# One root chain for the keys and the first query half, two longer root steps in place of three, a gate product over four heads, and a new issue order, in a two-layer attention trunk

## The chip, the cores and the metric

The kernel runs on one core of one Trainium2 chip. A core has five engines that run at once: TensorE multiplies matrices (PE in the profile, its weight loads PEld), VectorE (DVE), ScalarE (ACT) and GpSimd (POOL) work on tiles in the core's memory, and SyncE (SP) starts most of the transfers (DMA). Every engine takes its instructions from its own queue, in the order in which the program issued them; an instruction whose input is not there yet holds up everything behind it on that engine. The metric is the device time of one execution in microseconds (us). Three runs of the kernel before gave 298.65, 298.95 and 299.74 us; the median is 298.95.

## The reference

Two layers over 256 tokens of width 1024, 16 query heads and 4 key heads of 64 columns. Each layer takes shift, scale and gate from a condition vector, normalises x by its root mean square, makes queries, keys, values and z with one weight matrix, attends, multiplies by silu(z) and goes back through an output matrix:

```python
for i in range(DEPTH):
    shift, scale, gate = jnp.split(cond @ ada_w[i] + ada_b[i], 3, axis=-1)
    h = rms_norm(x, norm_g[i]) * (1 + scale[:, None, :]) + shift[:, None, :]
    y = nsa_mixer(h, ...) if i % 2 == 0 else moba_mixer(h, ...)
    x = x + gate[:, None, :] * y
...
def rms_norm(x, g):
    y = xf * lax.rsqrt(jnp.mean(xf * xf, axis=-1, keepdims=True) + NORM_EPS)
...
q = partial_rope(rms_norm(q.reshape(B, S, N_HEADS, HEAD_DIM), q_g), cos, sin)
k = partial_rope(rms_norm(k.reshape(B, S, N_KV, HEAD_DIM), k_g), cos, sin)
...
return (o * jax.nn.silu(z)) @ w_out
```

Layer 0 (nsa) has three kinds of keys: compressed blocks (a small network over 32-token windows), selected blocks and a window. With 256 tokens all four blocks are selected, so the last two are causal attention with different keys. Layer 1 (moba) is plain causal attention with one kind of key. Queries and keys are normalised per head of 64 columns, so every token needs one inverse square root for each head.

## The kernel before

The program does not call the engines directly. Every call to `T` (TensorE), `A` (ScalarE), `V` (VectorE), `G` (GpSimd) and `S`/`Q` (SyncE) is written down by `Plan.record` as an operation with a number, 2403 in all. `Plan.issue` then sends them out in the order of the list `ORDER`, which is written out by hand in the file; so a queue's order is the order of that engine's numbers in the list, and all instructions carry the line of the one call in `issue` (L303). Tiles have a tag (`buf`, `part`, `rs`, `g` and so on), and a tag has a fixed number of buffers which are handed out in that same order: a tile whose tag has no free buffer could not be issued there.

All large products are made in pairs of a rounded part and the rest of it (`part`, `HT`, `qg`, `KTA`): ScalarE copies the rounded part, VectorE subtracts to get the rest, and TensorE multiplies three of the four combinations. This subtraction is the largest use of VectorE.

The course of layer 0: the condition's products and the normalised x (0 to 15 us); keys and values of all three kinds with their weights arriving (15 to 80 us, `products_of`); then `make_k` for the selected and window keys, the tiles `FLAT` for the compressed keys (tile `p`, written by VectorE from transposed `KC`), and the products of FLAT with `nsa_cmp_w1` (`cmp_steps`), while `chunk` with `q_and_gates` makes the first eight query heads and the branch gates, and `make_q` turns the heads into `QT`; then the second query half, z, the attention of two pairs of key heads (`pair_a`), `gated` for each pair, and `out_products` with `w_out`. `next_h` (called per half of the tokens) makes h of layer 1. Layer 1 does the same with `make_k` for one kind of key, two `make_q`, z, `pair_b`, `gated` and the last `out_products`.

What the change touches:

`rstd_of(ss, n, inv)` makes an inverse square root out of small VectorE instructions on n columns: two that set up a first guess by bits, then three Newton steps, of three instructions each where n is over 1 and of two where n is 1. So a call has 11 or 8 instructions, and each needs the result of the one ahead of it.

`norm_rope` squares on ScalarE, sums each head on VectorE, calls `rstd_of`, scales and rotates. It is called by `make_k` in layer 0 (16 columns: 2 kinds, 2 token halves, 4 heads), by the first and second `make_q` (16 columns each), once for the compressed keys (1 column), and in layer 1 by `make_k` (8 columns) and two `make_q` (16 each). `rstd_of` with one column also runs twice at the start and twice in `next_h`.

`gated(pair, o, zT)` multiplies the attention output by z. `o` are four tiles in TensorE's output memory, one for each 32-token residue, holding four heads. It takes two heads at a time: four VectorE products into a tile `g` (128x128 each), one ScalarE copy and one VectorE subtraction into `qg`; then the same for the other two heads. `z_blocks` makes z as one `zT` tile for each two heads. The tag `g` has two buffers of 512 columns, `zT` four of 512, `rs` four of 64, `ss` four of 16.

Of the kernel before, what the change touches and what calls it, by code (L numbers as in the profile page):

```python
# [18 lines left out]
P = 128  # L19
# [318 lines left out]
def kernel(  # L338
# [46 lines left out]
    plan.tag("early", early["pool"], 1024, 12)  # L385
    plan.tag("buf", work, 1024, 10)
    plan.tag("part", work, 1024, 10, F32R)
    plan.tag("ss", work, 16, 4)
    plan.tag("rs", work, 64, 4)
    plan.tag("rot", work, 256, 1)  # L390
    plan.tag("rs2", early["pool"], 256, 1)
# [1105 lines left out]
```

## Time and profile before

| | |
|---|---|
| median of three runs | 298.95 us (298.65 to 299.74) |
| the profiled execution | 298.08 us, its span 296.3 us |
| granted TensorE clock | 1.000 |
| ACT busy | 194.6 us (66%) |
| POOL busy | 43.8 us (15%) |
| moved by DMA | 70.83 MB, mean 239 GB/s |

The span goes from the first to the last instruction; 1.78 us of the execution lie outside. An engine's busy time is the time in which at least one of its instructions was running. For TensorE the ends of matmuls are modelled and consecutive matmuls overlap, so it counts as busy a little past the moment at which it could have taken the next one. The profile's groups are named by tile: `rs` holds the root chains, `ss` the sums of squares, `p` is both FLAT and the attention's probabilities, `part` the split weights.

### The profile page before, as it was taken

What the parts mean: (1) busy time and instruction counts of PE and PEld (TensorE: products, weight loads), DVE (VectorE), ACT (ScalarE), POOL (GpSimd) and SP (SyncE); (2) the same over time, 40 slices, a digit from 0 to 9 for tenths busy, and PEclk for the clock granted to TensorE, in tenths of its full rate; (3) what the DMA queues carried; (4) which work ended last, traced back from release to release, by engine and by line L of the source; (5) the groups of instructions that cost most, each with busy time, mean ns of one, the idle gap of its engine ahead of it and who ended that gap; (6) DMA issues with size and microseconds to landing.
All of it is one profiled execution on the core that took longest, in us unless ns stands there. A gap on an engine that the chain in (4) does not pass through costs nothing. (4 is left out here: it accounts for less than half of the span.)

```text
span 296.3 us, 6988 instructions
## 1 busy us (share of the span) xinstructions
PE 286.2 (97%) x2612; PEld 240.8 (81%) x2612; DVE 255.2 (86%) x541; ACT 194.6 (66%) x464; POOL 43.8 (15%) x111
## 2 busy tenths in 40 slices
PE   6999999999989999999999999899999999999994
PEld 6877788799957878879997788678888999897874
DVE  0486899937899999999999999976889999999985
ACT  4283353649514669996899944877584899799410
POOL 8600889960000000000001000000000000000000
PEclk9999999999999999999999999999999999999999
DMA  7999999998939989797967989254878766295003
GB/s 236 318 334 349 352 364 340 357 295 269 318 117 368 385 280 364 231 291 160 270 194 214 227 210 347 89 177 145 283 283 215 204 171 195 74 237 154 2 0 142
DMA packets 48698, 70.83 MB, mean 239 GB/s; under 512 B 4919, under 2 KB 24985, under 8 KB 48666
## 3 DMA queue, kind: packets, MB, share of 16 engines
q1 hardware_dynamic: 48298, 70.34, 77.7%
q8 instruction: 20, 0.33, 0.5%
q14 instruction: 12, 0.10, 0.1%
q0 software_dynamic: 256, 0.02, 0.1%
q10 hardware_dynamic: 112, 0.04, 0.0%
HBM read 67.76 MB, written 2.62 MB: 238 GB/s over the span
## 5 line engine op out<-in xcount | busy, mean ns | idle before, releaser
L303 PE MATMUL ps<-part,HT 128*128 128x512 f32 (+2 forms) x408 | 96.2, 375 | 0.3
L303 PEld LDWEIGHTS ps<-part,HT 128*128 128x128 f32 x408 | 69.1, 188 | 13.0 <-issue 0.8
L303 DVE TENSOR_TENSOR part<-buf,part 128x1024 fp32r<-128x1024 f32 (+2 forms) x58 | 64.0, 1113 | 12.0 <-ACT part L303 10.1
L303 ACT CAST part<-buf 128x1024 fp32r<-128x1024 f32 (+2 forms) x58 | 55.4, 979 | 18.8 <-PE ps L303 11.5
L303 PE MATMUL ps<-HT,part 128*128 128x256 f32 x384 | 62.8, 289 | 0.0
L303 PEld LDWEIGHTS ps<-HT,part 128*128 128x128 f32 x384 | 52.8, 189 | 2.9 <-issue 0.9
L303 PE MATMUL ps<-part,qg 128*128 128x512 f32 (+1 forms) x240 | 49.1, 356 | 0.0
L303 PEld LDWEIGHTS ps<-part,qg 128*128 128x128 f32 x240 | 38.6, 188 | 8.4 <-issue 1.3
L303 ACT ACTIVATE p<-ps,tiny 128x256 f32<-128x256 f32 (+1 forms) x96 | 39.6, 459 | 7.4 <-DVE tiny L303 7.2
L303 PE MATMUL ps<-KTA,qg 128*128 128x256 f32 (+1 forms) x192 | 29.7, 288 | 0.5 <-ACT part L303 0.3
L303 ACT CAST part<-early 128x1024 fp32r<-128x1024 f32 (+1 forms) x16 | 15.0, 938 | 21.5 <-DMA early<-in_nsa_w_in_dram 21.4
L303 PEld LDWEIGHTS ps<-KTA,qg 128*128 128x128 f32 x192 | 25.8, 190 | 1.6 <-ACT part L303 0.4
L303 DVE TENSOR_REDUCE tiny<-ps 128x2 f32<-128x512 f32 (+2 forms) x40 | 24.8, 628 | 1.2 <-PE ps L303 1.0
L303 ACT ACTIVATION_READ_ACCUMULATOR p<-ps,tiny 128x1 f32 x96 | 23.4, 244 | 0.0
L303 DVE STREAM_TRANSPOSE p<-p 128x1536 f32<-128x1536 f32 x12 | 21.0, 1766 | 1.1 <-ACT p L303 0.9
L303 ACT ACTIVATE p<-p,tiny 128x256 f32<-128x256 f32 x48 | 21.8, 585 | 0.1
L303 ACT COPY buf<-ps 128x512 f32<-128x512 f32 (+1 forms) x25 | 11.7, 488 | 12.8 <-PE ps L303 10.1
L303 DVE TENSOR_TENSOR part<-early,part 128x1024 fp32r<-128x1024 f32 (+1 forms) x16 | 17.5, 1100 | 1.9 <-ACT part L303 1.9
L303 PE MATMUL ps<-buf,condz 128*32 128x256 f32 x192 | 11.8, 382 | 0.0
L303 DVE SCALAR_TENSOR_TENSOR sum<-early,condz,sum 128x512 f32<-128x512 f32 x14 | 10.6, 756 | 0.2
L303 POOL MEMSET buf<- 128x1024 f32 x1 | 1.0, 953 | 64.4 <-PE ps L303 64.4
L303 POOL TENSOR_SCALAR rot<-rot 128x16 f32<-128x16 f32 x19 | 10.1, 532 | 1.6
(191 smaller groups left out, 401.7 us busy)
## 6 DMA issues: line engine op xcount, KB each, us to landing
buf<-in_ada_w_dram SPq DMA_DIRECT2D x32, 512.0 KB, 5.7
buf<-in_moba_w_in_dram SPq DMA_DIRECT2D x20, 512.0 KB, 5.4
early<-in_ada_w_dram SPq DMA_DIRECT2D x32, 256.0 KB, 6.1
buf<-in_nsa_w_in_dram SPq DMA_DIRECT2D x12, 512.0 KB, 7.4
early<-in_nsa_w_in_dram SPq DMA_DIRECT2D x8, 512.0 KB, 5.8
buf<-in_nsa_cmp_w_dram SPq DMA_DIRECT2D x8, 512.0 KB, 5.7
buf<-in_nsa_w_out_dram SPq DMA_DIRECT2D x16, 256.0 KB, 8.7
buf<-in_moba_w_out_dram SPq DMA_DIRECT2D x16, 256.0 KB, 5.6
```

The lines of the kernel that those rows point to most:

```text
L303: getattr(self.engines[op["engine"]], method)(*[self._real(a) for a in args], **{k: self._real(a) for k, a in kw.items()})
```

## The change

Five things are edited, and since operations fall away, every number in `ORDER` after them is new; the list now has 2352 entries. The new list is not the old one renumbered: engine by engine it holds the same operations, less those removed, with many of them moved some places forward or back.

First, in `rstd_of` the three Newton steps become one Newton step and one third-order step: 9 instructions where n is over 1 and 7 where it is 1. The rows of the tile grow from 16 to 32 columns. Second, squaring and summing leave `norm_rope` (`square_sums`, `heads_of`), so that in layer 0 the sums of the keys (16 columns) and of the first query half (16) lie side by side in one `tiny` tile and one `rstd_of` call makes the roots of both; the keys are scaled only after that. In layer 1 the same is done with 8 and 16 columns. The second query halves keep a chain of their own. Third, `gated` makes its four products over all four heads (128x256 each) into one `g` tile, and `z_blocks` writes one `zT` tile for four heads. Fourth, the buffers follow: `ss` 2 of 16, `rs` 3 of 96, `zT` 2 of 1024, `g` 1 of 1024. Fifth, the order.

```diff
 ORDER = [
-    2, 1, 3, 0, 4, 49, 42, 43, 44, 51, 41, 48, 50, 45, 18, 19, 20, 21, 22, 16, 23, 24, 25, 26, 27, 28, 29, 30, 53,
...
+    1, 2, 18, 0, 3, 4, 42, 48, 44, 50, 43, 41, 49, 51, 19, 20, 21, 22, 23, 16, 24, 52, 54, 55, 53, 61, 62, 56, 63,
...
-    plan.tag("ss", work, 16, 4)
-    plan.tag("rs", work, 64, 4)
+    plan.tag("ss", work, 16, 2)
+    plan.tag("rs", work, 96, 3)
...
-    ATTN = {"qg": (1024, 4, F32R), "zT": (512, 4, F32), "p": (1536, 4, F32), "vr": (2048, 1, F32),
-            "u": (256, 1, F32), "pc": (256, 2, F32), "g": (512, 2, F32)}
+    ATTN = {"qg": (1024, 4, F32R), "zT": (1024, 2, F32), "p": (1536, 4, F32), "vr": (2048, 1, F32),
+            "u": (256, 1, F32), "pc": (256, 2, F32), "g": (1024, 1, F32)}
...
-        s = tile_of("rs", 3, 16)
-        half, y, a = (s[:q, i, :n] for i in range(3))
-        V.tensor_scalar(half, ss, 0.5 * inv, 0.5 * EPS, op0=OP.mult, op1=OP.add)
-        V.tensor_scalar(y.bitcast(I32), half.bitcast(I32), -0.5, float(1597463007 - 0x400000 - 2 ** 31), op0=OP.mult, op1=OP.add)
-        for _ in range(3):
+        s = tile_of("rs", 3, 32)
+        v, y, a = (s[:q, i, :n] for i in range(3))
+        V.tensor_scalar(v, ss, 64 / 9 * inv, 64 / 9 * EPS, op0=OP.mult, op1=OP.add)
+        V.tensor_scalar(y.bitcast(I32), v.bitcast(I32), -0.5, float(0x5f0b3000 - 2 ** 31), op0=OP.mult, op1=OP.add)
+        for step in range(2):
             if n == 1:
-                V.scalar_tensor_tensor(a, y, half, y, op0=OP.mult, op1=OP.mult)
+                V.scalar_tensor_tensor(a, y, v, y, op0=OP.mult, op1=OP.mult)
             else:
                 V.tensor_mul(a, y, y)
-                V.tensor_mul(a, a, half)
-            V.scalar_tensor_tensor(y, a, -1.5, y, op0=OP.add, op1=OP.mult)
+                V.tensor_mul(a, a, v)
+            if step:
+                V.scalar_tensor_tensor(a, a, -10 / 3, a, op0=OP.add, op1=OP.mult)
+            V.scalar_tensor_tensor(y, a, (-1.8898815748423101, 5.0)[step], y, op0=OP.add, op1=OP.mult)
         return y
...
+    def square_sums(src, dst, ss):
+        A.activation(dst, src, AF.Square)
+        V.tensor_reduce(ss, dst, axis=AX.X, op=OP.add)
+
-    def norm_rope(src, nm, nh, tabC, tabS, dst):
+    def norm_rope(src, nm, nh, tabC, tabS, dst, r):
...
-        A.activation(dst, src, AF.Square)
-        ss = tile_of("ss", 16)[:q, :n]
-        V.tensor_reduce(ss, dst, axis=AX.X, op=OP.add)
-        r = rstd_of(ss, n, 1.0 / HD)
...
-        for acc in accs:
-            t, zT = tile_of("y", 2, S), tile_of("zT", 2, S)
+        zT = tile_of("zT", 4, S)
+        for q, acc in enumerate(accs):
+            t = tile_of("y", 2, S)
             A.activation(t, acc, AF.Tanh, scale=0.5)
-            V.scalar_tensor_tensor(zT, t, 1.0, acc, op0=OP.add, op1=OP.mult)
-            out.append(zT)
+            V.scalar_tensor_tensor(zT[:, 2 * q:2 * q + 2], t, 1.0, acc, op0=OP.add, op1=OP.mult)
+        out.append(zT)
...
+    def heads_of(raw, ss):
+        y = tile_of("buf", ss.shape[1], HD)
+        square_sums(raw, y, ss)
+        return raw, y
...
     def gated(pair, o, zT):
+        t = tile_of("g", 4, S)
+        for a in range(4):
+            sl = [z.rearrange("p j (b i) -> p j b i", b=8)[:, :, a:8 - a:7 - 2 * a] for z in (t, zT[pair])]
+            V.tensor_mul(sl[0], sl[1], o[a].rearrange("p (m h i) -> p h m i", m=2, h=4))
         for q in range(2):
-            t = tile_of("g", 2, S)
-            for a in range(4):
-                sl = [z.rearrange("p j (b i) -> p j b i", b=8)[:, :, a:8 - a:7 - 2 * a] for z in (t, zT[2 * pair + q])]
-                V.tensor_mul(sl[0], sl[1], o[a].rearrange("p (m h i) -> p h m i", m=2, h=4)[:, 2 * q:2 * q + 2])
+            some = t[:, 2 * q:2 * q + 2]
             both = tile_of("qg", 2, 2, S)
...
-            A.copy(both[:, :, 0, :], t)
-            V.tensor_sub(both[:, :, 1, :], t, both[:, :, 0, :].bitcast(F32))
+            A.copy(both[:, :, 0, :], some)
+            V.tensor_sub(both[:, :, 1, :], some, both[:, :, 0, :].bitcast(F32))
...
-    make_k(raw_k, (2, 3), KTA, (256, 384, 128, 0))
+    sums = tile_of("tiny", 32)
+    k_own = k_heads(raw_k, sums[:, 0:16])
...
-    make_q(raw_q, 0, QT, 0)
+    q_own = q_heads(raw_q, sums[:, 16:32])
+    roots = rstd_of(sums, 32, 1.0 / HD)
+    make_k(k_own, roots[:, 0:16], (2, 3), KTA, (256, 384, 128, 0))
+    make_q(q_own, roots[:, 16:32], 0, QT, 0)
...
-    make_k(raw_k, (5,), KTB, (0, P))
+    sums = tile_of("tiny", 32)
+    k_own = k_heads(raw_k, sums[:, 0:8])
...
-    make_q(raw_q, 4, QT, 0)
+    q_own = q_heads(raw_q, sums[:, 8:24])
+    roots = rstd_of(sums[:, 0:24], 24, 1.0 / HD)
+    make_k(k_own, roots[:, 0:8], (5,), KTB, (0, P))
+    make_q(q_own, roots[:, 8:24], 4, QT, 0)
```

More of the change, by code (lines that the diff above doesn't have):

```diff
@@ L803, in raw_part, with k_heads, q_heads, make_k @@
         return done
-    def make_k(raw_k, kinds, kt_view, offs):
+    def heads_of(raw, ss):
+        y = tile_of("buf", ss.shape[1], HD)
+        square_sums(raw, y, ss)
+        return raw, y
+    def k_heads(raw_k, ss):
+        return heads_of(raw_k.rearrange("p c m (g d) -> p (c m g) d", d=HD), ss)
+    def q_heads(raw_q, ss):
+        return heads_of(raw_q.rearrange("p m (h d) -> p (m h) d", d=HD), ss)
+    def make_k(heads, r, kinds, kt_view, offs):
         n = len(kinds)
-        src = raw_k.rearrange("p c m (g d) -> p (c m g) d", d=HD)
-        y = tile_of("buf", 8 * n, HD)
+        src, y = heads
         k0, j0 = kinds[0], (2, 3, 5).index(kinds[0])
         norm_rope(src, 2 * n, KVH, TC[:, j0:j0 + n].rearrange("p c m d -> p (c m) d"),
-                  TS[:, k0:k0 + n].rearrange("p c m d -> p (c m) d"), y)
+                  TS[:, k0:k0 + n].rearrange("p c m d -> p (c m) d"), y, r)
         for j, off in enumerate(offs):
@@ L825, in make_k, with make_q @@
             V.tensor_sub(lo, tv, hi.bitcast(F32))
-    def make_q(raw_q, kind, qt, g0):
-        y = tile_of("buf", 16, HD)
-        norm_rope(raw_q.rearrange("p m (h d) -> p (m h) d", d=HD), 2, 8, TR[:, kind], TS[:, kind], y)
+    def make_q(heads, r, kind, qt, g0):
+        src, y = heads
+        norm_rope(src, 2, 8, TR[:, kind], TS[:, kind], y, r)
         for m in range(2):
@@ L1103 @@
     A.copy(raw_q[:, :, 0:256], q_acc)
-    KC = [[tile_of("zT", KVH, 2 * HD) for m in range(2)] for kv in range(2)]
+    KC = [[both[:, m] for m in range(2)] for both in (tile_of("zT", 2, KVH, 2 * HD) for kv in range(2))]
     for ci in (1, 2, 0):
@@ L1210 @@
     kcy = const.tile([64, 1, HD], F32, name="kcy")
-    norm_rope(kcm[:, None, 0:64], 1, 1, TCc[:, None, :], TSc[:, None, :], kcy)
+    sums = tile_of("tiny", 32)[0:64, 0:1]
+    square_sums(kcm[:, None, 0:64], kcy, sums)
+    norm_rope(kcm[:, None, 0:64], 1, 1, TCc[:, None, :], TSc[:, None, :], kcy, rstd_of(sums, 1, 1.0 / HD))
     kcz = tile_of("part", 1, 2, 2, HD)
@@ L1238, in second_q @@
         chunk(w_in, ((512, 512),), raw_part(raw_q, 512))
-        make_q(raw_q, 0, QT, 2)
+        sums = tile_of("tiny", 32)[:, 0:16]
+        own = q_heads(raw_q, sums)
+        make_q(own, rstd_of(sums, 16, 1.0 / HD), 0, QT, 2)
     SECOND = -1
@@ L1419 @@
     chunk(m_in, ((0, 512),), raw_part(raw_q, 512))
-    make_q(raw_q, 4, QT, 0)
+    q_own = q_heads(raw_q, sums[:, 8:24])
+    roots = rstd_of(sums[:, 0:24], 24, 1.0 / HD)
+    make_k(k_own, roots[:, 0:8], (5,), KTB, (0, P))
+    make_q(q_own, roots[:, 8:24], 4, QT, 0)
     raw_q = tile_of("buf", 2, 512)
     chunk(m_in, ((512, 512),), raw_part(raw_q, 512))
-    make_q(raw_q, 4, QT, 2)
+    sums = tile_of("tiny", 32)[:, 0:16]
+    own = q_heads(raw_q, sums)
+    make_q(own, rstd_of(sums, 16, 1.0 / HD), 4, QT, 2)
     zT = []
```

241 rows, old and new, of the table ORDER are left out of this document.

## The prediction, made before the changed kernel ran

> **What bounds the kernel now.** I read the page's busy times first, then the stages, then what TensorE waits for.
>
> ```profile
> span 296.3 us, 6988 instructions
> ...
> PE 286.2 (97%) x2612; PEld 240.8 (81%) x2612; DVE 255.2 (86%) x541; ACT 194.6 (66%) x464; POOL 43.8 (15%) x111
> ```
>
> TensorE is busy for all but 10.1 us, VectorE for all but 41. The change takes no work from TensorE, so it can only shorten TensorE's waits. Where they lie, a cut of the span into stages says (stage and length; then busy us and instructions of PE, PEld, DVE, ACT, POOL; granted clock; DMA share; GB/s):
>
> ```profile
> 0.00:10.00 10.00, 7.70 (x35) 7.38 (x36) 3.01 (x19) 4.40 (x7) 8.62 (x40) 1.00 0.86 250
> 10.00:70.00 60.00, 59.17 (x425) 48.52 (x424) 43.93 (x86) 30.30 (x46) 33.80 (x70) 1.00 1.07 343
> 70.00:100.00 30.00, 28.47 (x196) 22.60 (x195) 27.79 (x70) 15.04 (x25) 0.40 (x1) 1.00 0.81 270
> 100.00:185.00 85.00, 84.85 (x1141) 71.72 (x1140) 81.51 (x173) 69.14 (x211) 0.95 (x1) 1.00 0.88 259
> 185.00:200.00 15.00, 14.11 (x66) 10.49 (x65) 12.60 (x43) 11.94 (x30) 0.00 (x0) 1.00 0.41 137
> ...
> 215.00:260.00 45.00, 44.48 (x409) 40.49 (x409) 43.01 (x97) 35.55 (x85) 0.00 (x0) 1.00 0.67 191
> 260.00:290.00 30.00, 29.97 (x259) 24.82 (x259) 28.84 (x43) 18.01 (x46) 0.00 (x0) 1.00 0.35 91
> 290.00:296.30 6.30, 2.41 (x17) 2.05 (x15) 3.14 (x7) 0.00 (x0) 0.00 (x0) 1.00 0.46 166
> ```
>
> Of the 10.1 us, 2.30 lie in the first 10 us and 3.89 at the end, where the result is written out. The middle has 3.95: 0.83 while the first weights arrive, 1.53 between 70 and 100, 0.15 in layer 0's attention, 0.89 between the layers, 0.52 between 215 and 260, next to nothing after. In the third and the sixth stage VectorE is 93% and 96% busy: there the two are nearly even.
>
> The busy figure hides part of the waits, because a matmul counts as busy past the start of the next one:
>
> ```profile
> 83.22 0.40 PE L303 MATMUL ps<-part,HT 128*128 128x512 f32 x1
> ...
> 84.94 4.19 PE L303 MATMUL ps<-buf,p 128*64 128x256 f32 x32 [1.32 <-DVE p L303]
> ...
> 89.99 2.00 PE L303 MATMUL ps<-part,HT 128*128 128x512 f32 x8
> ...
> 93.48 0.48 PE L303 MATMUL ps<-part,HT 128*128 128x512 f32 x1
> ...
> 94.17 0.63 PE L303 MATMUL ps<-identF,y 128*128 128x128 f32 x4 [0.21 <-DVE p L303]
> ```
>
> The eight at 89.99, each 0.40 long, start (2.00 - 0.40) / 7 = 0.23 us apart. After the one at 83.22 the next starts 1.72 us later, so 1.49 us are lost, and 1.32 show. After the one at 93.48 it is 0.69, so 0.46 are lost and 0.21 show. Both wait for VectorE's additions into FLAT (tile `p`). I therefore take the lost time in the middle to be up to twice what shows, 7.9 us.
>
> The Trainium skill (Perfetto Trace Analysis, section Identifying the Most-Contended Engine) goes further: matmul busy time is a poor measure of distance from the limit, weight-load busy time a better one. By that rule (81% against VectorE's 86%) VectorE would be the limit and every microsecond taken from it would count; that is the first rival. The two places above speak for the rule, the 10 to 70 row (PE 59.17 of 60, DVE 43.93) against it.
>
> **The change part by part.** VectorE's groups (count, busy us, mean ns of one):
>
> ```profile
> L303 DVE TENSOR_TENSOR g<-zT,ps 128x128 f32<-128x128 f32 x32 | 7.0, 278 | 1.0 <-PE ps L303 1.0
> ...
> L303 DVE TENSOR_TENSOR rs<-rs 128x16 f32<-128x16 f32 x30 | 4.9, 169 | 0.5
> L303 DVE SCALAR_TENSOR_TENSOR rs<-rs 128x1 f32<-128x1 f32 x24 | 4.2, 186 | 0.5
> ...
> L303 DVE TENSOR_TENSOR y<-ps,buf 128x256 f32<-128x256 f32 x4 | 1.7, 420 | 0.2
> ...
> L303 DVE TENSOR_TENSOR rs<-rs 128x8 f32<-128x8 f32 x6 | 1.0, 165 | 0.1
> ...
> L303 DVE TENSOR_TENSOR tiny<-ps,GBIAS 128x48 f32<-128x48 f32 x2 | 0.4, 204 | 0.0
> ```
>
> *Merged chains.* A chain on 16 columns is 11 instructions of about 0.169 us, 1.86 us. In layer 0 two of them (3.72) become one of 9 on 32 columns. That width is not in the trace: it lies between 0.169 (16 columns) and 0.204 (48 columns, read from TensorE's memory). I take 0.18, nearer to the first, as going from 8 to 16 columns costs only 0.004: 1.62, so 2.1 us less (bounds 1.88 and 2.20). In layer 1, 11 x 0.165 and 11 x 0.169 are 3.67; 9 at 0.175 are 1.58, also 2.1 less (1.83 to 2.15).
>
> *Shorter chains.* The two second query halves lose 2 x 0.169 each, 0.68 together. Five one-column chains (two at the start, two in `next_h`, one for the compressed keys) lose one instruction of 0.186 each, 0.93.
>
> *Gate.* Per pair of key heads:
>
> ```profile
> 174.12 9.53 PE L303 MATMUL ps<-part,qg 128*128 128x512 f32 x47
> 174.19 1.67 DVE L303 TENSOR_TENSOR g<-zT,ps 128x128 f32<-128x128 f32 x8 [0.38 <-PE ps L303]
> ...
> 175.30 0.62 ACT L303 CAST qg<-g 128x512 fp32r<-128x512 f32 x1 [3.98 <-DVE g L303]
> 175.96 0.69 DVE L303 TENSOR_TENSOR qg<-g,qg 128x512 fp32r<-128x512 f32 x1
> ```
>
> Eight products take 1.67 us: 0.28 each, 0.08 of it overlapping the next. Four of twice the size at 0.42 take 1.44 with that overlap and 1.68 without: 0.2 us less per pair, 0.8 over four pairs (bounds 0 and 0.9). The first copy into `qg` now waits for all four products: it started 1.11 us after the first product and will start about 1.5 after. TensorE covers the 0.4: it runs 9.53 us without a break from before the products to long after the copy. Behind the waiting copy on ScalarE stand casts of weights for the same output products, under the same cover; without it, it costs 0.4 a pair. The single `g` buffer makes the next pair's products wait for this pair's last subtraction (0.69 each), but the pairs lie far apart, so I cost it at nothing.
>
> *VectorE in all*: 2.1 + 2.1 + 0.68 + 0.93 + 0.8 = 6.6 us: 0.37 at the start, 3.0 between 70 and 185, 0.37 between the layers, 2.84 after 215.
>
> *What reaches TensorE.* Between 71 and 85 us six instructions of the keys' chain stand in VectorE's queue ahead of the additions for which TensorE waits at 84.94 (the keys' sums are ready from 71 on, row below). All go to the merged chain: 6 x 0.169 = 1.0 us of the 1.49; next late is the query half's sum, which stays. Of the 0.46 at 93.48 I take 0.3. From 100 to 185 0.15 us shows idle and VectorE saves 0.9; I take 0.3. Between the layers the chain of `next_h` stands alone on the path:
>
> ```profile
> 188.01 1.05 DVE L303 SCALAR_TENSOR_TENSOR rs<-rs 128x1 f32<-128x1 f32 x5
> ...
> 191.37 0.50 PE L303 MATMUL ps<-KTA,HT 128*128 128x512 f32 x1 [0.88 <-ACT HT L303]
> ```
>
> Five dependent steps take 1.05, so one fewer gives 0.2. From 220 to 240 the chain that ended last runs through VectorE piece by piece (start, length, what; its first root step, one of the middle, and the first score maximum after them):
>
> ```profile
> 220.18 0.16 DVE rs L303
> ...
> 236.35 0.19 DVE rs L303
> ...
> 238.51 0.69 DVE tiny L303
> ```
>
> There VectorE saves 2.4, but TensorE shows only 0.52 idle, at most 1.0 by the doubling: I take 0.8. At the start I take 0.1, because the next stage moves 343 GB/s at a DMA share of 1.07 and its products follow the weights. At the end nothing changes. Sum: 1.0 + 0.3 + 0.3 + 0.2 + 0.8 + 0.1 = 2.7 us.
>
> *The new order* is the unknown. Renumbering the diff's list shows the same 1225 TensorE entries, on average 7 places from where they were and at most 66, so it reshuffles within stages. No row shows its waits. On the good side it is bounded by the 7.9 us lost in the middle; on the bad side by new waits of the size of the largest now, 1.49: three of them would be 4.5. I take zero, since most stretches of either list are the same products in another sequence.
>
> The execution profiled took 298.08 us, so 295.4 after; it lay 0.87 below the median of the runs, 298.95, so **296.2** for the median.
>
> **Rivals.** *VectorE is the bound* and its savings land whole: 6.6 less the 0.37 at the start, 298.95 - 6.2 = 292.7. For it speak the waits on `p` and the chain from 220 to 240; against it 84.85 of 85 us in layer 0's attention.
>
> *TensorE was full*: freed VectorE time turns into idle VectorE time, and a wait that goes comes back behind the next instruction (ScalarE's casts, the weights). Only `next_h` and a little else is gained, 0.5: 298.5, no change by measurement. For it speaks the 97%; against it the 1.49 us, which have a plain cause. A change that did not do what it says would look the same; VectorE's count (541, to be 51 fewer) tells them apart.
>
> *Keys wait for queries*, the slower one. The keys' roots now need the sums of the first query half. In layer 0 sums and scalings stood so, keys first, then queries:
>
> ```profile
> 71.40 1.22 DVE L303 TENSOR_REDUCE ss<-buf 128x16 f32<-128x1024 f32 x1 [0.24 <-ACT buf L303]
> ...
> 82.59 1.20 DVE L303 TENSOR_REDUCE ss<-buf 128x16 f32<-128x1024 f32 x1
> ...
> 87.42 1.21 DVE L303 TENSOR_TENSOR buf<-buf,rs 128x1024 f32<-128x1024 f32 x1
> ...
> 94.36 1.23 DVE L303 TENSOR_TENSOR buf<-buf,rs 128x1024 f32<-128x1024 f32 x1
> ```
>
> Queued behind the merged chain are the keys' rotation, their transposes and the splits into `KTA`, and the scores wait for those. If the keys slip to the queries' place, all this is 6.9 us late. If TensorE covers a third, 4.6 are lost against 1.4 gained elsewhere (0.3 + 0.2 + 0.8 + 0.1): 302.2. It decides once the uncovered delay is over 1.4 us. Against it: the query sums are ready at 83.79, nine steps of 0.2 end near 86, before the keys' scaling at 87.42 now.
>
> **How the numbers follow.** Two such kernels can be told apart from about 0.5%, 1.5 us: faster means under 297.45, slower over 300.45. Chances: forecast 0.45 (a gain of 1.5 to 5), VectorE bound 0.14, TensorE full 0.27, keys late or another wait of the new order 0.14. So faster 0.59, same 0.27, slower 0.14. The range leaves out most of the slower rival and a little below the first: 292.4 to 300.5.
>
> **What would show it.** VectorE with 490 instructions and about 249 us busy; `rs` rows of 32 and 24 columns below 0.2 us; 16 `g` rows of 128x256; TensorE's wait on `p` ahead of the first product with FLAT under 0.6 us; the wait on `HT` between the layers 0.2 shorter. I am wrong if TensorE's idle time in the middle stays near 3.95 us, if new waits on `KTA` or `qg` appear, or if the weights' stage ends at another time than 70 us.

## The result and the profile after

The changed kernel took 302.01 us (median of seven runs, 300.39 to 304.22) and the kernel before 298.45 (297.64 to 299.74): the ratio is 1.0128, 95% interval 1.0089 to 1.0166. It is slower, by 2.7 to 5.0 us, where 2.7 us less were forecast. In some runs of every kernel TensorE stands at half its clock for a window of 3.41 us, which costs about 1.7 us (an estimate, half of the window); five of the seven runs here had one, and the two without took 300.39 and 301.69, so this explains at most a part. The profiled execution took 301.69 us, its span 300.0.

The page of the changed kernel, its busy times:

```profile
span 300.0 us, 6944 instructions
...
PE 287.7 (96%) x2612; PEld 241.9 (81%) x2612; DVE 249.9 (83%) x490; ACT 194.6 (65%) x464; POOL 43.6 (15%) x111
```

VectorE has lost its 51 instructions and 5.3 us of busy time. TensorE does the same 2612 products and is idle longer. The same cut into stages as before (stage and length; busy us and instructions of PE, PEld, DVE, ACT, POOL; granted clock; DMA share; GB/s):

```profile
10.00:70.00 60.00, 59.75 (x431) 48.99 (x431) 43.19 (x80) 31.92 (x49) 33.63 (x70) 1.00 1.03 333
70.00:100.00 30.00, 28.46 (x196) 23.17 (x196) 26.88 (x57) 12.87 (x23) 0.40 (x1) 1.00 0.88 302
100.00:185.00 85.00, 82.15 (x1112) 68.52 (x1111) 76.22 (x155) 68.47 (x209) 0.95 (x1) 1.00 0.84 249
185.00:200.00 15.00, 13.82 (x71) 10.55 (x70) 13.48 (x43) 10.09 (x26) 0.00 (x0) 1.00 0.33 117
...
215.00:260.00 45.00, 44.50 (x394) 39.99 (x393) 43.24 (x76) 36.37 (x83) 0.00 (x0) 1.00 0.71 182
```

The third row is the one to see. Layer 0's attention showed 0.15 us of idle TensorE before and shows 2.85 now, while VectorE's load there fell from 81.51 to 76.22. In the other rows TensorE's idle time differs by 0.6 us at most. VectorE's groups of the change (count, busy us, mean ns of one) came out as priced:

```profile
L300 DVE TENSOR_TENSOR g<-zT,ps 128x256 f32<-128x256 f32 x16 | 5.9, 415 | 2.0 <-PE ps L300 1.8
...
L300 DVE TENSOR_TENSOR rs<-rs 128x32 f32<-128x32 f32 x4 | 0.7, 185 | 0.1
L300 DVE TENSOR_TENSOR rs<-rs 128x24 f32<-128x24 f32 x4 | 0.7, 181 | 0.1
```

Where did TensorE stop? Its timeline, the rows behind a wait (start, length, what, and in brackets the idle time and what ended it; "issue" is a wait for nothing that the profile shows):

```profile
84.96 3.74 PE L300 MATMUL ps<-buf,p 128*64 128x256 f32 x32 [1.54 <-DVE p L300]
...
139.99 0.50 PE L300 MATMUL ps<-HT,part 128*128 128x256 f32 x2 [0.88 <-ACT part L300]
...
161.22 1.93 PE L300 MATMUL ps<-buf,condz 128*32 128x256 f32 x32 [0.33 <-issue]
...
172.53 0.45 PE L300 MATMUL ps<-p,vr 32*64 32x128 f32 x8 [1.22 <-issue]
...
194.78 0.50 PE L300 MATMUL ps<-part,HT 128*128 128x512 f32 x1 [0.79 <-ACT HT L300]
...
196.31 0.51 PE L300 MATMUL ps<-KTA,HT 128*128 128x512 f32 x1 [0.34 <-DVE HT L300]
```

Taken from start to start, as in the prediction, these lose 1.71, 1.23, 0.58, 1.46, 0.94 and 0.50 us. The first was 1.49 before, the last two were one of 1.03, the other three are new: 1.23 + 0.58 + 1.46 + 0.22 + 0.41 = 3.90, against a span that is 3.7 longer. (The sum does not close exactly: the products with the second half of FLAT start 0.73 us earlier than before, at 94.23, and some smaller waits are longer.)

The wait at 139.99 is for a cast on ScalarE, and that cast has a row of its own:

```profile
138.90 2.00 ACT L300 CAST part<-buf 128x1024 fp32r<-128x1024 f32 x2 [2.37 <-DMA buf<-in_nsa_w_in_dram]
```

It waited 2.37 us for z weights. SyncE's queue, which starts the loads (start, time in the queue's engine, what, count):

```profile
120.31 0.39 SPq L300 DMA_DIRECT2D buf<-in_ada_w_dram  x1
120.79 0.42 SPq L300 DMA_DIRECT2D buf<-in_nsa_w_in_dram  x1
121.30 0.42 SPq L300 DMA_DIRECT2D buf<-in_ada_w_dram  x1
...
128.36 0.46 SPq L300 DMA_DIRECT2D buf<-in_nsa_w_in_dram  x1
141.23 1.92 SPq L300 DMA_DIRECT2D buf<-in_nsa_w_out_dram  x3
```

By their numbers in the list, the load at 128.36 is the one that is needed first, at 139; the condition weights at 120.31 and 121.30 are used only at 162 and 161. The next load was issued at 141.23, just after VectorE's subtraction had read the first of the late weights (141.20), so none starts for 13 us. Before, the same z weights were asked for at 122.73 and used at 135.7:

```profile
122.73 0.37 SPq L303 DMA_DIRECT2D buf<-in_nsa_w_in_dram  x1
```

### The profile page after: what moved, and what is told of

It reads as the page before. It is cut to its first block, busy times and chain, and to the rows that moved or that the text cites. A ratio compares the mean times of both kernels' runs of the same rounds, so it can differ in the third digit from the quotient of the medians.

```text
span 300.0 us, 6944 instructions
## 1 busy us (share of the span) xinstructions
PE 287.7 (96%) x2612; PEld 241.9 (81%) x2612; DVE 249.9 (83%) x490; ACT 194.6 (65%) x464; POOL 43.6 (15%) x111
## 5 line engine op out<-in xcount | busy, mean ns | idle before, releaser
L300 PE MATMUL ps<-part,HT 128*128 128x512 f32 (+2 forms) x408 | 97.3, 375 | 0.8 <-ACT HT L300 0.8
L300 PEld LDWEIGHTS ps<-part,HT 128*128 128x128 f32 x408 | 68.3, 188 | 12.9 <-ACT HT L300 1.7
L300 PE MATMUL ps<-HT,part 128*128 128x256 f32 x384 | 65.4, 291 | 0.9 <-ACT part L300 0.9
L300 PEld LDWEIGHTS ps<-HT,part 128*128 128x128 f32 x384 | 53.7, 190 | 4.4 <-ACT part L300 1.2
L300 ACT ACTIVATION_READ_ACCUMULATOR p<-ps,tiny 128x1 f32 x96 | 24.7, 258 | 0.0
L300 ACT ACTIVATE p<-p,tiny 128x256 f32<-128x256 f32 x48 | 22.6, 603 | 0.1
L300 ACT COPY buf<-ps 128x512 f32<-128x512 f32 (+1 forms) x25 | 12.3, 517 | 12.4 <-PE ps L300 12.4
L300 PE MATMUL ps<-p,vr 32*64 32x128 f32 (+1 forms) x368 | 10.1, 298 | 1.4 <-issue 1.4
```

Of the source, the lines that this page charges most:

```text
L300: getattr(self.engines[op["engine"]], method)(*[self._real(a) for a in args], **{k: self._real(a) for k, a in kw.items()})
```

## The experiments

Two questions: is it the edits or the order, and what in the order? The kernels were timed in five sets, each on a chip of its own with the kernel before beside them (298.17 to 298.47 us); the ratios are to that one. A median is known to about 1 us.

**The edits alone**, with the old order. The old list is renumbered, the removed numbers left out, and the merged chains stand where the queries' chain stood.

```diff
 ORDER = [
-    1, 2, 18, 0, 3, 4, 42, 48, 44, 50, 43, 41, 49, 51, 19, 20, 21, 22, 23, 16, 24, 52, 54, 55, 53, 61, 62, 56, 63,
+    2, 1, 3, 0, 4, 49, 42, 43, 44, 51, 41, 48, 50, 45, 18, 19, 20, 21, 22, 16, 23, 24, 25, 26, 27, 28, 29, 30, 53,
...
```

> The changed kernel's four edits of the code with the instruction order of the kernel before: its list renumbered, the removed entries left out, the merged root chains where the queries' chain stood; 50 of the 2352 entries stand elsewhere only because their inputs would not be ready. If the new order is what costs (theory O), the slow-down of 3.6 us goes and what the edits alone gain is seen: 295.8 to 298.5 us, at or a little below the kernel before (298.45), with the new waits at 139 and 171 us gone. If the edits cost (theory E: the keys wait for the queries' sums, the single g buffer), the time stays near the changed kernel's 302 us whatever the order.

298.68 us, ratio 1.0006 (0.9976 to 1.0035), just above the range of theory O and far from theory E. Page and TensorE's timeline of this kernel:

```profile
PE 285.8 (96%) x2612; PEld 240.1 (81%) x2612; DVE 251.1 (85%) x490; ACT 194.7 (66%) x464; POOL 44.1 (15%) x111
```

```profile
84.64 4.13 PE L294 MATMUL ps<-buf,p 128*64 128x256 f32 x32 [0.77 <-DVE p L294]
...
93.63 0.66 PE L294 MATMUL ps<-identF,y 128*128 128x128 f32 x4 [0.72 <-ACT y L294]
```

The slow-down is gone, so it was the order. But nothing is gained either: the wait at FLAT fell from 1.49 to 0.94 us lost, and the next one, at the products that turn the keys (`identF,y`), rose from 0.46 to 0.89. It moved as well: before it was the second group of them (94.17), put down to an addition into FLAT (`p`), now it is the first, which follows ScalarE's copy of the rotated keys (`y`).

**The new order with the old code.** The removed operations are put in beside those that they belong to (the keys' chain directly ahead of the queries'). In the file of the kernel before:

```diff
 ORDER = [
-    2, 1, 3, 0, 4, 49, 42, 43, 44, 51, 41, 48, 50, 45, 18, 19, 20, 21, 22, 16, 23, 24, 25, 26, 27, 28, 29, 30, 53,
+    1, 2, 18, 0, 3, 4, 42, 48, 44, 50, 43, 41, 49, 51, 19, 20, 21, 22, 23, 16, 24, 52, 54, 55, 53, 62, 63, 56, 64, 65,
...
```

> The code of the kernel before (two chains of three Newton steps, gate by two heads) with the changed kernel's order, the operations that the change removed put in beside the ones they belong to. Theory O: 302 to 304 us, as slow as the changed kernel or a little slower, with the waits at 139 and 171 us still there. Theory E: back near 298.5 us.

307.39 us, ratio 1.0303 (1.0254 to 1.0351): slower than foreseen. What TensorE waited for in this kernel (us in total, times, longest):

```profile
PE ps L297 <- DVE part L297: 2.6, 2, 2.0
PE ps L297 <- issue: 2.0, 2, 1.8
PE ps L297 <- ACT part L297: 1.8, 1, 1.8
```

The waits for `part` on ScalarE and for "issue" are the two of the changed kernel, and longer; the first row is new. So in this order old code and edits are 307.39 - 302.01 = 5.4 us apart, and in the old one not measurably. The 5.4 are not the worth of the edits alone, since a part hangs on where the removed operations were put: the longest new wait, 2.05 us at 83.77, ends with a remainder that VectorE began at 82.50, behind the keys' chain as it was put in (from 80.26 on); in the changed kernel that remainder began at 80.27.

**The late load.** Two entries of SyncE's queue are exchanged.

```diff
-    1325, 1076, 1117, 1073,
+    1325, 1028, 1117, 1073,
...
-    1075, 1028,
+    1075, 1076,
```

> The changed kernel with two entries of the order exchanged: the load of the z weights that are needed at 139 us takes the place of a load of condition weights that are needed only at 162 us, and the reverse, so it is issued about 8 us earlier. Theory O, its first part (late z weights): the wait of ScalarE for that load (2.37 us) and TensorE's wait of 1.23 us behind it go, the hole in the DMA traffic from 135 to 141 us closes, and the time falls by 1.2 to 2.0 us to 300.0 to 300.8. Rival: TensorE only meets the next late thing, the time stays within 0.5 us of 302.

301.45 us, ratio 1.0103 (1.0066 to 1.0140). TensorE's timeline:

```profile
138.24 0.58 PE L295 MATMUL ps<-HT,part 128*128 128x256 f32 x2
...
160.23 1.93 PE L295 MATMUL ps<-buf,condz 128*32 128x256 f32 x32 [1.05 <-issue]
```

The wait of 1.23 us is gone as foreseen, but the products with the condition weights now lose 1.29 us where they lost 0.58. TensorE came 1.7 us sooner, and they started only 1.0 us sooner: 0.7 us were given back 20 us later. The time lies between the two expectations, and its interval overlaps that of the changed kernel (1.0089 to 1.0166); the hole in the loads did not close either, with none issued from 128.4 to 139.7. What the trace shows is the wait that went and the one that grew.

**The row of small products.** Nine output products are moved between the two value groups. (In the trace the row of small products counts 136, from 168.59 to 172.71 us, and 68 stand on either side of the nine; the 34 of the recorded texts are the products of one entry of the list.)

```diff
+    1366, 1388, 1367, 1389, 1368, 1369, 1370, 1390, 1391,
     1299,
...
-    1366, 1388, 1367, 1389, 1368, 1369, 1370, 1390, 1391,
```

> The changed kernel with nine 512-wide output products moved, in TensorE's order, from behind to between two groups of 34 small value products at 168 to 173 us, as the kernel before had seven there. Theory F (a long row of small matmuls runs ahead of the fetch of TensorE's instructions): the 1.22 us in which TensorE waited at 171 us for nothing that the profile shows go, and the time falls by 0.8 to 1.3 us to 300.7 to 301.2. Rival: the stall sits at that place for another reason (a semaphore that the profile does not name), it moves with the group, and the time stays within 0.5 us of 302.

300.97 us, ratio 1.0069 (1.0032 to 1.0106). The wait at 171 us is gone, and 1.0 us of the median with it, as theory F has it (the interval still overlaps that of the changed kernel). The counter-test does the reverse to the kernel before (old numbers):

```diff
-    1393, 1415, 1416, 1394, 1395, 1396, 1417,
     1321,
+    1393, 1415, 1416, 1394, 1395, 1396, 1417,
```

> The kernel before with its seven output products between the two groups of 34 small value products (168.9 to 170.7 us) moved behind the second group, so that the groups follow each other as in the changed kernel; nothing else. Theory F (TensorE runs out of instructions, since the block it needs is fetched behind the data transfers): a wait of about 1.4 us in the second group, put down to no releaser, appears, ended some 1.4 us after the block of instructions has landed, and the time is 1.0 to 1.5 us above before, 299.2 to 299.7. Rival: the stall belongs to something else in the changed kernel, and the time stays within 0.4 us of 298.2.

300.01 us, ratio 1.0060 (1.0029 to 1.0091), 0.3 us more than theory F had, and TensorE's timeline has the wait:

```profile
171.45 0.50 PE L297 MATMUL ps<-p,vr 32*64 32x128 f32 x12
173.29 0.45 PE L297 MATMUL ps<-p,vr 32*64 32x128 f32 x9 [1.34 <-issue]
```

It stands in the middle of a row of like products of which twelve had run, so a missing input is unlikely. Counting TensorE's instructions in the trace from the start, beginning with 0, it stands ahead of number 3265 here, and ahead of the same number in the changed kernel, in the one with the early load and in the old code with the new order. The trace also has the packets that bring instructions (queue 8; packets, MB, share), for the changed kernel as a whole and from 170.0 to 171.2 us:

```profile
q8 instruction: 20, 0.33, 0.5%
```

```profile
q1 hardware_dynamic: 233, 0.44, 99.6%
q8 instruction: 1, 0.02, 5.5%
```

Twenty blocks of 16 KB for 5289 instructions of TensorE are 264 for each. In the four kernels that wait, a block landed at 171.16, 170.37, 174.65 and 171.64 us, and TensorE went on at 172.53, 171.76, 176.19 and 173.29: 1.37 to 1.65 us later each time. In the kernel before, the block landed at 169.96 and TensorE came to number 3265 at 171.63, 1.67 us later, without a wait: the seven products between the groups had given the time. The other blocks say the same: counting on from number 3265 in steps of 256, both ways, the first instruction of a block started 1.29 us or more after its block had landed, in each of the 19 blocks that this reaches, in all fourteen traces; in steps of 255 or 257 the shortest time is 1.02 or 0.68. So TensorE runs out of instructions there. A smaller shortage stands in both kernels, at number 2241: in the changed one 0.48 us at 137.27, 1.35 after a landing, and in the kernel before 0.53 at 135.73, 1.41 after a landing. That the block comes late because the data transfers fill the DMA engines (99.6% in the row above) is argued, not shown; its packet took 1.05 us there, and 0.98 us at 278.95, where the DMA share is 0.06, so if they delay it, they delay its start and not the packet itself.

**Three places mended.** The two changes above, and the condition products (1074, 1077) put behind seven and three more output products:

```diff
-    1164, 1074, 1077,
+    1164,
...
+    1379, 1074,
...
+    1351, 1077,
```

> The changed kernel with three places of its order mended together: the exchange of the two loads (z weights early), the nine output products between the two value groups, and the two groups of condition products that waited at 159 to 161 us put behind seven and three output products more. Theory O, in these places: 302.0 less 1.2 (139 us) less 1.2 (171 us) less 0.6 (160 us), that is 298.7 to 299.3. Rival: with these three gone the same time is lost in other places, the time stays over 300.5.

299.29 us, ratio 1.0035 (1.0007 to 1.0063), as theory O has it. Of the 3.33 us between the changed kernel and the edits in the old order, 2.72 are these three places.

**Why do the edits bring nothing in the old order?** The remaining waits were filled with ready products, with the old code and with the edits. In both (new numbers):

```diff
+    766, 774, 775, 767, 768, 769, 770,
     548,
...
+    1888, 1889, 1890, 1891, 1884, 1898,
     2055,
...
+    1988, 1998, 1992,
     2123,
```

> The kernel before, its code unchanged, with the same three moves of TensorE's products (not the move in VectorE's queue). If the moves do all and the edits nothing: 296.7 to 297.5, at most 0.7 us above the edits with the same moves. If VectorE's saving of 4 to 5 us is worth something once the order lets it: 1.0 us or more above that kernel. If TensorE is full: 298.2, no change.

298.48 us, ratio 0.9999 (0.9971 to 1.0027). TensorE's timeline:

```profile
85.19 3.97 PE L297 MATMUL ps<-buf,p 128*64 128x256 f32 x32
...
92.98 0.66 PE L297 MATMUL ps<-identF,y 128*128 128x128 f32 x4 [1.29 <-DVE rs L297]
```

The 1.49 us at FLAT are gone, and 1.46 are lost six microseconds later, for the keys; their second group goes on losing 0.5 as before. With the edits, the same moves and VectorE's chain ahead of the additions for the second half:

> The edits with the order of the kernel before (298.68) and moves at three places: seven output products ahead of the first product with FLAT, where TensorE waits 0.94 us at 83.5; VectorE's merged chain and the keys' rotation ahead of the additions for the second half of FLAT, for TensorE's wait of 0.89 us for the keys at 92.5; six and three products of ready weights ahead of scores that wait 0.61 us at 236.2 and 0.49 us at 252.9. If such waits are real losses that order can fill: 296.0 to 297.0. If TensorE is full and each wait that goes comes back behind the next instruction: within 0.5 us of 298.7.

299.82 us, ratio 1.0028 (0.9994 to 1.0062), in neither range; the profiled execution, at full clock throughout, took 298.58. TensorE's timeline:

```profile
85.21 3.67 PE L294 MATMUL ps<-buf,p 128*64 128x256 f32 x32
...
98.30 0.44 PE L294 MATMUL ps<-identF,g 128*128 128x128 f32 x2 [0.47 <-ACT g L294]
99.13 0.54 PE L294 MATMUL ps<-identR,part 128*128 128x128 f32 x4 [0.15 <-DVE part L294]
...
103.02 0.63 PE L294 MATMUL ps<-pc,u 128*128 128x64 f32 x4 [0.27 <-ACT buf L294]
```

Both waits are gone, and TensorE is 2.0 us ahead of the kernel before at 95 us. At 105 it is 0.2 ahead: the compressed keys' chain is late instead. Fourteen z products were then put into these gaps:

> The kernel with the edits in the old order and the three moves, and now fourteen output products of ready z weights put ahead of the four places between 97 and 103 us where the 2 us that it was ahead at 95 us were given back (waits of 0.72, 0.40 and 0.43 us for the compressed keys' chain and the queries). If the loss at 97 to 103 us is only a lack of filling: 1.2 to 1.8 us below that kernel, 296.3 to 297.0 in undisturbed runs, below before. If the chain through VectorE sets the end of this stage, the wait moves to the first scores at 105 us and the time stays within 0.5 us.

298.99 us, ratio 1.0017 (0.9988 to 1.0046). In its timeline one wait is left before the scores:

```profile
104.21 0.63 PE L294 MATMUL ps<-pc,u 128*128 128x64 f32 x4 [0.48 <-ACT buf L294]
```

This execution lost 1.4 us early to a window of half clock; against that it held some 0.9 us of its lead to 160 us and lost it by 195. No version beat the kernel before.

**The same in the mended new order.** There TensorE waits 1.7 us at FLAT because an addition stands behind three entries for the second half. VectorE's timeline of the changed kernel, the last addition that TensorE needs (84.48) and two of those ahead of it, and then the edit in VectorE's entries:

```profile
83.20 0.09 DVE L300 MEMSET p<- 128x32 f32 x1
...
83.75 0.38 DVE L300 TENSOR_TENSOR p<-ps,RT 64x224 f32<-64x224 f32 x1
...
84.48 0.43 DVE L300 TENSOR_TENSOR p<-ps,RT 64x256 f32<-64x256 f32 x1
```

```diff
-    536, 647, 523, 648, 531, 521, 640, 649, 524, 650, 651, 525,
+    523, 525, 647, 648, 649, 650, 651, 652, 653, 654, 655, 657, 658, 656, 659, 536, 531, 521, 524,
```

> The mended new order (299.29) with three moves on VectorE: between 82 and 92 us the last two additions for the first half of FLAT, then the merged root chain and the keys' rotation, ahead of the additions for the second half (TensorE waits 1.70 us at 83.5 for an addition that stands behind three of the second half); at 238 us the keys' remainder ahead of a sum of squares (0.54 us); at 194 us one remainder of h ahead of another (0.50 us). If these waits are an order's fault and the time behind them is free: 299.29 less 1.7 to 2.7, that is 296.6 to 297.6, below before. If VectorE or TensorE is full in that stage, the wait comes back before 105 us and the time is 298.5 to 299.3.

305.45 us, ratio 1.0238 (1.0209 to 1.0267), a miss of its own making:

```profile
89.74 1.62 PE L295 MATMUL ps<-buf,p 128*64 128x256 f32 x6 [4.92 <-DVE p L295]
```

TensorE did not go on after the last addition it reads (525, ended at 83.67) but 0.06 us after the addition 531 of the other half, in the same tile, which had been moved back. Second form:

> The same as new_order_mended_moves, but the addition 531 of the second half stays where it was, ahead of the chain, and the other additions of the second half are issued after the first product with FLAT, so that TensorE's wait cannot cover them. There TensorE had waited 5.08 us at 84.4 us and gone on 0.06 us after that addition. If the wait at FLAT was an order's fault and the time behind it is free: the mended new order (299.29) less 1.5 to 2.5, that is 296.8 to 297.8, below before. If the stage from 70 to 105 us is bound by VectorE's chain as in the old order with moves: TensorE is ahead at 90 us and has given back most of it by 105, 298.3 to 299.3.

304.00 us, ratio 1.0163 (1.0122 to 1.0204). The first half met no wait, the second did:

```profile
86.66 3.67 PE L295 MATMUL ps<-buf,p 128*64 128x256 f32 x32
98.82 1.76 PE L295 MATMUL ps<-buf,p 128*64 128x256 f32 x7 [3.08 <-DVE KTA L295]
```

The releaser named there is a guess of the profile. SyncE's queue in the same kernel:

```profile
84.80 10.92 SPq L295 DMA_DIRECT2D buf<-in_nsa_cmp_w_dram  x4
```

The four loads of the weights for these products stretch over 10.92 us. The third was issued at 94.80, when VectorE's scaling of the queries had ended (94.78): the order had given it a buffer that came free only there. It landed at 98.68, 0.14 before TensorE went on. Third form:

> The third form of these moves. In the second TensorE met no wait at the first half of FLAT any more, but waited 3.33 us at 95.25 us for the second half: the load of its weights had been given a buffer that came free only with the queries' scaling at 94.77 us. Here the queries' scaling and rotation are issued behind the first eight products with FLAT, so that this load gets the buffer it had in the mended new order, free at 87 us. Free time behind the wait: 299.29 less 1.5 to 2.5, 296.8 to 297.8, below before. A stage bound by VectorE's chain: TensorE is 1.5 us or more ahead at 90 us and has given back most of it by 105, and the time is 298.3 to 299.3.

299.57 us, ratio 1.0033 (1.0006 to 1.0060), as without the moves:

```profile
95.13 3.74 PE L295 MATMUL ps<-buf,p 128*64 128x256 f32 x32 [0.79 <-DMA buf<-in_nsa_cmp_w_dram]
```

The 1.70 us are gone and 1.04 lost again 10 us on, now for weights of the second half that landed at 95.08. SyncE had issued that load at 90.03, behind one that it could issue only at 89.55, when VectorE's rotation of the keys had ended (89.52); without the moves that one was issued at 87.45. So the moved chain made the weights late. The range of the mended kernel without a move, 298.95 to 300.91, and of this one, 298.68 to 301.11, cover each other.

## Why the prediction was wrong

*VectorE's saving.* Right, step by step: a chain instruction on 32 columns takes 0.185 us (0.18 taken), on 24 columns 0.181 (0.175), a gate product 0.415 (0.42). The `rs` rows add up to 17.8 us before and 12.2 after, the `g` rows to 7.0 and 5.9: together 6.7, where 6.6 were forecast. VectorE's busy time fell by less, 5.3 us (4.1 with the edits in the old order).

*What reaches TensorE.* Wrong: 2.7 us were forecast, and the edits alone gave 0.2 us more, with an interval from 0.7 less to 1.0 more. The step that failed is "1.0 us of the 1.49; next late is the query half's sum, which stays". What was late next was the keys' rotation behind the merged chain: 0.55 came off, 0.43 went on 10 us later. Nor did the 0.8 between 220 and 240 come: the wait there was 0.44 us before and 0.61 with the edits alone. I read "up to twice what shows, 7.9 us" as time to be won; in five kernels a wait that was taken away was met again, in part or whole, within 20 us.

*The new order at zero.* This is the step with the size: the order costs 3.33 us by the medians (302.01 against 298.68), and mending three places of it gives back 2.72. The reason given, "most stretches of either list are the same products in another sequence", is true and says nothing. An order that moves a load by a few entries changes when the weights arrive, and one that puts two groups of small products together changes whether TensorE's next instructions are there in time. The bound of three waits of 1.49, 4.5 us, did hold it; I should have read the loads in the renumbered list against the products that use them, which needs no chip.

*Rivals.* The slower rival has its chance for "keys late or another wait of the new order", and the second half is what came. That its 302.2 is so near 302.01 is luck, since it was added up from keys that are late by 6.9 us; the keys' delay is there but small (0.43 us). "TensorE was full", 298.5, is what the edits do in the old order (298.68), by its words: a wait that goes comes back. "VectorE is the bound" fails in the old order; in the new one old code and edits are 5.4 us apart, but 2.05 of them are a wait that comes from where the keys' chain was put, and what the edits alone are worth there stays open. The Trainium skill's rule (Perfetto Trace Analysis, section Identifying the Most-Contended Engine), by which weight loading at 81% left VectorE as the limit, would have given 292.7; with the edits in the old order VectorE fell from 255.2 to 251.1 us and the time stayed.

*The single `g` buffer and the gate.* In the changed kernel TensorE has no wait on `qg` or `g`; both cost nothing, as taken.

*The signs.* The count of 490, the rows on 32 and 24 columns and the 16 `g` rows were seen; the wait on `p` under 0.6 us was not (1.54), nor the shorter wait between the layers (1.44 lost in two places against 1.03). TensorE's idle time between 10 and 290 us, whose staying near 3.95 was to show the forecast wrong, rose to 6.3.

## What to carry to other kernels

A change of the issue order is priced by its loads and its instruction stream too: for every load that moves, compare its new place in the queue with the first use of its data, and look for rows of small products that have lost the large ones between them where a new block of instructions is due. Where two engines are both nearly full, time saved on one is worth what the order lets through, here nothing that could be measured in the old order; measure edits and order apart. A wait of 1 us on a full engine is a gain only if what comes behind it is early by as much, so follow the next two waits before counting it.

## What the runs showed of the hardware

TensorE can run out of instructions. In four kernels a row of 136 small value products, 68 of which take about 1.3 us, was held up by 1.46 to 2.07 us at the same instruction of the stream, until 1.37 to 1.65 us after a block of instructions had landed. The length of the row is not enough: the kernel before runs 172 such products in a row (170.73 to 173.92 us) without this wait, because its blocks had landed in time. The Trainium skill (Runtime: NRT & Kernel Launch, section Instruction fetch mechanics) describes refills in blocks of 16 KiB or 256 instructions, which the twenty blocks and the steps of 256 here bear out, and calls the crossing of a block mostly hidden; with these rows it is not.

TensorE's clock falls to half for windows of 3.41 us. In the first two forms of the last experiment such windows fall into or directly behind the long waits (5.08 and 3.33 us lost); the stages of the first form, then of the second, with the granted clock as the third number from the end:

```profile
84.00:87.00 3.00, 0.82 (x6) 0.39 (x4) 2.66 (x9) 0.99 (x1) 0.00 (x0) 1.00 0.72 235
87.00:94.00 7.00, 4.26 (x21) 3.12 (x23) 6.66 (x18) 1.14 (x2) 0.00 (x0) 0.51 0.28 78
```

```profile
99.00:102.40 3.40, 3.40 (x18) 2.41 (x17) 1.52 (x3) 0.00 (x0) 0.00 (x0) 0.50 1.06 378
```

The Trainium skill (TensorE: Matmul & The Clock Gate, Part 1) has the clock halved after an idle window of about 3.4 us. Here less was enough: in the first form the clock fell at 87.07 us, 2.25 us into the wait, in the second behind a wait of 3.08 us, with TensorE busy for 0.33 of the 3.41 us ahead of the window. Other windows do not fit at all: seven traces had one or two that began between 8 and 21 us or, in the kernel before with the groups joined, at 138.78, and in the 3.41 us ahead of each TensorE was busy for 1.47 us or more, at 138.78 for 3.01. And in the old code with the new order TensorE was busy for only 1.65 us from 141.06 to 144.47, and the granted clock stayed at 1.00 behind it. What sets these windows off stays open. Of 35 runs of the kernel before, ten with a mean granted clock of 0.994 or less took 299.3 to 301.0 us and the others 297.5 to 299.3.
